# The last stage of a decoder layer on token tiles instead of feature chunks, and u blocks that end earlier

## The chip, the cores and the metric

One core of a Trainium2 chip runs the whole kernel. The metric is the device time of one execution in microseconds. The kernel before takes 2055.36 us (median of 3 runs, 2055.13 to 2056.61).

## What is computed

One step of one decoder layer for 544 tokens (512 of a prompt, 8 samples of 4) with 1024 features, all in 32-bit floats. Cut to what matters here:

```
x = x + merged @ w_out                      # two mixers, merged by gates
x = x + peer_ffn(rmsnorm(x, g_ffn), peer_wq, peer_keys, expert_u, expert_v)
ple_gate = sigmoid(rmsnorm(x, g_ple) @ w_ple_gate)   # 1024 x 1024
x = x + (p @ w_ple) * ple_gate                       # p: 544 x 256, w_ple: 256 x 1024
y = rmsnorm(x, g_final)
```

peer_ffn picks, for each token and each of 8 heads, the best 16 of 128 x 128 experts by two lists of 128 scores, and adds gate * gelu(h . u) * v over the picked rows of expert_u and expert_v.

## The kernel before, in words

**Numbers.** A product of two 32-bit matrices is three passes of TensorE over a high and a low part. `split` (L122 to L124) makes the parts: ScalarE (ACT) copies the high one (L123), VectorE (DVE) subtracts it (L124). A weight row that is loaded takes a raw buffer, then a high and a low one, in rings (`wload`, L128).

**Layout.** Up to the end, x lies with features on partitions: `x1` is 128 x 8 x 544, eight chunks of features. The sums of the experts lie with tokens on partitions.

**Stages, in us of the span.** Until about 657 the mixers, their merge and w_out. From there one block, "peer", whose order on every engine is set by a planner of the toolchain that plays the program through with its own costs (`schedule_with_timeline_sim`); the order below is what it made, and the engines run it strictly in that order.

1. *Queries and choice.* x1 is written to DRAM (`x1s`, five DMAs of POOL, L871), since its memory is reused. The norm of x1 (g_ffn) is split; 16 query columns wq are multiplied (`pj`, L917), turned into scores `psc` (L938), copied by ACT (`sc`, L939), and DVE takes the best 16 (`top16`). 16 transposes `ph` make token rows `htok` and `hsam` (L903 to L908). The transposes and the scores share two PSUM buffers (tag "mx"). Then DVE chooses among the pairs (`select`) and makes the gates with TensorE (`oa`, `ob`, `pg`, L1070 to L1088); the gates go to DRAM and come back as `gg`.
2. *Experts of the first 384 tokens, densely.* A u block multiplies 128 rows of expert_u by the normed x (24 matmuls `pu`, L967 to L970); 65 such blocks are made early, 63 late. The main loop has 128 steps j: a step loads one block of expert_v (`vraw`), splits it (`whi`, `wlo`) and the weights (`wgh`, `wgl`), and adds 18 matmuls of 512 columns into `pacc` (L1195), which fills six PSUM banks. The late u blocks are spread over the steps by `nlate * (j + 1) / LATE`, LATE = 127.
3. *Experts of the other 160 tokens, by gathered rows.* 320 times POOL gathers one row per token into one of 4 buffers `rows` (L1109) and DVE multiplies it (L1117, `jk`) or adds it (L1127, `accg`: `accs[0]` for 128 tokens, `accs[1]` for the samples). The steps lie between those of the main loop.
4. *The last stage.* x1 comes back from DRAM. The sums of each token tile are copied by ACT (`ot`, L1257), transposed in groups of four by TensorE (`pt`, L1250) and added to x1 (L1252); `accs` too, the samples by a small matmul with `sel` (L1289). Then, for two halves of 272 tokens: norm with g_ple (squares on ACT, their sum over partitions by TensorE, `pn`), eight chunks c with 24 matmuls each (`pj`, L1304: weights stationary, 272 tokens moving), sigmoid, times `pw` = p @ w_ple (L1266), added to x1; then the final norm and four output DMAs. Each w_ple_gate chunk is loaded and split twice, once for each half (16 loads).

Of the kernel before, what the change touches and what calls it, by code (L numbers as in the profile page):

```python
# [56 lines left out]
def step_kernel(ctx: ExitStack, tc: tile.TileContext, xT, pT, pk, wab, win, wbr, wout, wq, keysT, eu, eur, ev,  # L57
                wple, wpg, sh, sd, scv, yT, o_hp, o_dp, o_cv, o_hs, o_ds, gdram, ysp, gsp, x1s, asp, usp):
# [1172 lines left out]
    def tile_(tag, bufs, shape, dt=F32):
        return lp.tile(shape, dt, name=tag, tag=tag, bufs=bufs)

    yo0 = [tile_("yo", NYO, [128, 2, HT]) for _ in range(2)]
    tile_("xn3", NXN, [128, HT])
    tile_("sg2", 2, [128, HT])
    ph = tile_("fh", 2, [128, 2, T], F32R)
    pl = tile_("fl", 2, [128, 2, T], F32R)
    NRAW, NHI = TW
    wp = wr = tail.enter_context(tc.tile_pool(name="wpt", bufs=2, side="right", reuse_waits="tile"))  # L1240
    wpl = [wload(wple[i]) for i in range(2)]

    for k in range(2):
        nc.sync.dma_start(yo0[k].rearrange("p a b -> p (a b)"), pT[:, k])
        split(ph[:, k], pl[:, k], yo0[k].rearrange("p a b -> p (a b)"))

    def residual(t, ot, k0):
        p = psu.tile([128, 512], F32, name="pt", tag="pu").rearrange("p (a b) -> p a b", a=4)
        for k in range(4):
            PE.transpose(p[:, k], ot[:, k * 128:(k + 1) * 128], ident)  # L1250
        xc = x1[:, k0:k0 + 4, t * 128:(t + 1) * 128]
        V.tensor_add(xc, xc, p)  # L1252

    for t in range(3):
        for k0 in range(0, 8, 4):
            ot = ots[k0 // 4]
            S.activation(ot, pacc[t][:, k0 // 4], AF.Copy)  # L1257
            residual(t, ot, k0)
    for c in range(8):
        wh, wl = wpl[c // 4]  # L1260
        for hf in range(2):
            p = psu.tile([128, 512], F32, name="pw", tag="pu")
            for k in range(2):
                w_ = 2 * (c % 4) + k
                for j, (a, b) in enumerate(((wh, ph), (wh, pl), (wl, ph))):
                    PE.matmul(p[:, :HT], a[:, w_], b[:, k, HS[hf]], start=(k == 0 and j == 0), stop=(k == 1 and j == 2))  # L1266
            S.activation(pw[:, c, HS[hf]], p[:, :HT], AF.Copy)
# [1 line left out]
    psj = tail.enter_context(tc.tile_pool(name="psj2", bufs=4, space=PSUM, reuse_waits="tile"))
    pn = tail.enter_context(tc.tile_pool(name="pn2", bufs=2, space=PSUM, side="right", reuse_waits="tile"))  # L1270


    def norm(i):
        xs = x1[:, :, HS[i]]
        r = rms_rstd(x2p, pn.tile([128, 512], F32, name="pn", tag="pn").rearrange("p (a b) -> p a b", a=1),
                     lambda k: xs[:, k], 8, 0)
        return xs, r

    parts = []
    for i in range(2):  # L1280
        if i == 1:
            for k0 in range(0, 8, 4):
                residual(3, accs[0][:, k0 * 128:k0 * 128 + 512], k0)
            for k0 in range(0, 8, 4):
                p = psu.tile([128, 512], F32, name="pts", tag="pu")[:, :4 * NS].rearrange("p (a b) -> p a b", a=4)
                for k in range(4):
                    PE.matmul(p[:, k], accs[1][:, (k0 + k) * 128:(k0 + k + 1) * 128], sel, start=True, stop=True)
                xc = x1[:, k0:k0 + 4, TP:]
                V.tensor_add(xc, xc, p)  # L1289
        xs, r2 = norm(i)  # L1290
        hh = tile_("fh", 2, [128, 8, HT], F32R)
        hl = tile_("fl", 2, [128, 8, HT], F32R)
        for k in range(8):
            xn = tile_("xn3", NXN, [128, HT])
            V.scalar_tensor_tensor(xn, xs[:, k], par("g_ple", k), r2, op0=OP.mult, op1=OP.mult)
            split(hh[:, k], hl[:, k], xn)
# [104 lines left out]
```

## Time and profile before

| what | us |
|---|---|
| median of 3 runs | 2055.36 (2055.13 to 2056.61) |
| the profiled execution, its own time | 2064.72 |
| its span | 2062.6 |
| PE, DVE, ACT, POOL busy | 1982.7, 1702.2, 1031.5, 516.3 |
| last product of the main loop ends | 1946.6 |
| from there to the end of the span | 116.0 |

PE is TensorE's matmuls, PEld its weight loads, SP the engine that issues most DMAs. In a timeline a row gives start, duration, engine, line, operation, the tile written and those read, and what ended the idle time before it. A matmul's duration holds its way through the array, so the pace is the distance between starts. Where a group waits, the engine named behind the arrow is the one whose result came last.

### The profile page before, as it was taken

What the parts mean: (1) busy time and instruction counts of PE and PEld (TensorE: products, weight loads), DVE (VectorE), ACT (ScalarE), POOL (GpSimd) and SP (SyncE); (2) the same over time, 40 slices, a digit from 0 to 9 for tenths busy, and PEclk for the clock granted to TensorE, in tenths of its full rate; (3) what the DMA queues carried; (4) which work ended last, traced back from release to release, by engine and by line L of the source; (5) the groups of instructions that cost most, each with busy time, mean ns of one, the idle gap of its engine ahead of it and who ended that gap; (6) DMA issues with size and microseconds to landing.
All of it is one profiled execution on the core that took longest, in us unless ns stands there. A gap on an engine that the chain in (4) does not pass through costs nothing.

```text
span 2062.6 us, 34654 instructions
## 1 busy us (share of the span) xinstructions
PE 1982.7 (96%) x12292; PEld 1838.5 (89%) x12292; DVE 1702.2 (83%) x4579; ACT 1031.5 (50%) x1720; POOL 516.3 (25%) x509
## 2 busy tenths in 40 slices
PE   6899999999999999999999899999999999999887
PEld 6898988989998999999999888888888888888777
DVE  7687978876566799999999789888888788887877
ACT  5657576663534446765666433333333333333354
POOL 0001010010100001213332255543343344454510
PEclk9999999989999999999999999999999999999978
DMA  4323443434755238999999899999999999999843
GB/s 165 108 103 137 149 151 124 166 139 167 266 196 199 70 100 199 252 263 347 384 379 349 279 353 352 338 354 342 343 341 335 343 339 357 323 335 321 319 147 125
DMA packets 189420, 518.86 MB, mean 252 GB/s; under 512 B 18608, under 2 KB 72240, under 8 KB 189120
## 3 DMA queue, kind: packets, MB, share of 16 engines
q1 hardware_dynamic: 132384, 311.70, 42.8%
q0 software_dynamic: 56864, 204.96, 29.2%
q8 instruction: 96, 1.57, 0.3%
q14 instruction: 76, 0.62, 0.1%
HBM read 455.80 MB, written 60.79 MB: 250 GB/s over the span
## 4 chain that ended last, share of the span: by engine, by line
PE 83%; DVE 5%; DMA 4%; issue 3%; ACT 2%; POOL 1%; SPq 0%; DVEq 0%; ACTq 0%; POOLq 0%
PE pacc L1195 23%; PE pj L166 14%; PE pu L968 8%; PE pu L967 8%; PE pu L970 8%; PE pj L917 5%; PE pg L1084 4%; PE pj L1304 2%; DMA lraw<-in_eu 1%; DMA rows<-in_ev,idxs 1%; PE pmb L554 1%; PE pma L349 1%; PE pmb L545 1%; DMA usp<-lraw 1%; POOL rows L1109 1%
## 5 line engine op out<-in xcount | busy, mean ns | idle before, releaser
L967 PE MATMUL pu<-hh,whi 128*128 128x384 f32 x1024 | 346.1, 338 | 2.6 <-ACT act L978 2.6
L968 PE MATMUL pu<-hl,whi 128*128 128x384 f32 x1024 | 345.7, 338 | 0.0
L1109 POOL DMA_INDIRECT rows<-in_eur,idxs x160 | 215.0, 1344 | 291.5 <-DVE jk L1117 258.4
L124 DVE TENSOR_TENSOR wlo<-wraw,whi 128x1024 fp32r<-128x1024 f32 x169 | 206.3, 1221 | 76.0 <-ACT whi L123 66.1
L123 ACT ACTIVATE whi<-wraw 128x1024 fp32r<-128x1024 f32 x169 | 178.5, 1057 | 162.8 <-PE pj L166 85.1
L1109 POOL DMA_INDIRECT rows<-in_ev,idxs x160 | 203.2, 1270 | 226.4 <-DVE accg L1127 189.6
L1127 DVE SCALAR_TENSOR_TENSOR accg<-rows,wts,accg 128x1024 f32<-128x1024 f32 x158 | 202.2, 1280 | 14.5 <-DMA rows<-in_ev,idxs 14.1
L1195 PE MATMUL pacc<-whi,wgl 128*128 128x512 f32 x768 | 197.5, 392 | 5.3 <-DVE wgl L124 5.2
L970 PE MATMUL pu<-hh,wlo 128*128 128x384 f32 x1024 | 202.4, 336 | 0.0
L967 PEld LDWEIGHTS pu<-hh,whi 128*128 128x128 f32 x1024 | 192.5, 188 | 6.0 <-ACT act L978 3.6
L1195 PE MATMUL pacc<-whi,wgh 128*128 128x512 f32 x768 | 196.6, 391 | 0.2 <-ACT wgh L123 0.2
L1195 PE MATMUL pacc<-wlo,wgh 128*128 128x512 f32 x768 | 196.2, 391 | 0.0
L968 PEld LDWEIGHTS pu<-hl,whi 128*128 128x128 f32 x1024 | 192.4, 188 | 2.4
L124 DVE TENSOR_TENSOR wlo<-vraw,whi 128x1024 fp32r<-128x1024 f32 x128 | 156.5, 1223 | 34.5 <-ACT whi L123 29.3
L123 ACT ACTIVATE whi<-vraw 128x1024 fp32r<-128x1024 f32 x128 | 133.9, 1053 | 98.8 <-PE pacc L1195 72.2
L166 PE MATMUL pj<-xh,whi 128*128 128x272 f32 x768 | 176.6, 304 | 4.2 <-ACT sg L692 2.8
L970 PEld LDWEIGHTS pu<-hh,wlo 128*128 128x128 f32 x1024 | 178.7, 188 | 0.1
L1195 PEld LDWEIGHTS pacc<-whi,wgl 128*128 128x128 f32 x768 | 144.8, 189 | 37.2 <-DVE wgl L124 6.1
L166 PE MATMUL pj<-xh,wlo 128*128 128x272 f32 x768 | 175.4, 302 | 0.5 <-DVE wlo L124 0.5
L166 PE MATMUL pj<-xl,whi 128*128 128x272 f32 x768 | 174.4, 301 | 0.2 <-DVE xl L124 0.2
L1195 PEld LDWEIGHTS pacc<-wlo,wgh 128*128 128x128 f32 x768 | 144.9, 189 | 30.2
L1195 PEld LDWEIGHTS pacc<-whi,wgh 128*128 128x128 f32 x768 | 143.3, 188 | 27.0 <-ACT wgh L123 0.5
(488 smaller groups left out, 4326.0 us busy)
## 6 DMA issues: line engine op xcount, KB each, us to landing
wraw<-in_eu SPq DMA_DIRECT2D x128, 512.0 KB, 6.4
vraw<-in_ev SPq DMA_DIRECT2D x128, 512.0 KB, 6.4
wraw<-in_win SPq DMA_DIRECT2D x48, 512.0 KB, 3.6
gg<-gdram SPq DMA_DIRECT2D x25, 768.0 KB, 8.0
gdram<-go SPq DMA_DIRECT2D x36, 512.0 KB, 9.4
lraw<-in_eu SPq DMA_DIRECT2D x34, 512.0 KB, 4.0
usp<-lraw SPq DMA_DIRECT2D x34, 512.0 KB, 2.6
wlo<-usp SPq DMA_DIRECT2D x34, 512.0 KB, 7.7
```

What stands on the lines that cost most here:

```text
L123: S.activation(hi, src, AF.Copy)
L124: return V.tensor_sub(lo, src, hi.bitcast(F32))
L166: PE.matmul(ps[:, hf, :HT], a, b[:, HS[hf]], start=(i == 0 and j == 0), stop=(i == n - 1 and j == 2))
L917: PE.matmul(p[:, i, :HT], w_[:, k], x_[:, k, :HT], start=(k == 0 and j == 0), stop=(k == 7 and j == 2))
L967: PE.matmul(ps[:, :ND], wh[:, k], hh[:, k], start=(k == 0), stop=False)
L968: PE.matmul(ps[:, :ND], wh[:, k], hl[:, k], start=False, stop=False)
L970: PE.matmul(ps[:, :ND], wl[:, k], hh[:, k], start=False, stop=(k == 7))
L1084: PE.matmul(p[:, j], A[:, j], B[:, j], start=True, stop=True)
L1109: G.indirect_dma_start(out=r, out_offset=None, in_=src, in_offset=bass.IndirectOffsetOnAxis(ap=idx, axis=0))
L1127: V.scalar_tensor_tensor(accs[i], r, wts[i][:, k:k + 1], accs[i], op0=OP.mult, op1=OP.add)
L1195: PE.matmul(pacc[t][:, hf], w_[:, ts], v_[:, hf * 512:(hf + 1) * 512], start=(j == 0 and i == 0), stop=(j == 127 and i == 2))
L1304: PE.matmul(ps, a[:, k], b[:, k], start=(k == 0 and j == 0), stop=(k == 7 and j == 2))
```

## The change

It has three parts. Constants: LATE is 110 (the late u blocks are spread over steps 0 to 109, and the last 17 steps are products alone), and the last stage's weights have a ring of two raw buffers (TW = 2).

In the first stage x1 is written to DRAM with tokens on partitions: 40 transposes `px` into the "mx" buffers, ten ACT copies into `htok` or `hsam` (which are free until the token rows are made), ten DMAs of POOL.

In the last stage five tiles of tokens (128, 128, 128, 128, 32) are worked on, with features along the free axis. The sums are added to x1 straight from PSUM or from `accs`; a norm's sum of squares comes from one ACT operation with an accumulator; the normed tile is transposed in two groups of four and split; the normed tokens are stationary, and rows of w_ple and w_ple_gate of 512 columns move. Each of the ten weight rows is loaded and split once and kept. The norms run two tiles ahead of the outputs; there are five output DMAs; g_ple and g_final come as rows of 1 MB (`grow`).

```diff
-LATE = 127
+LATE = 110
-TW = 3, 2
+TW = 2
...
-    for t in range(5):
-        G.dma_start(x1s[t, :, :, :min(128, T - t * 128)], x1[:, :, t * 128:min(T, t * 128 + 128)])
...
+    for t in range(5):
+        n = min(128, T - t * 128)
+        for i in range(2):
+            p = pst.tile([128, 4, 128], F32, name="px", tag="mx")
+            for k in range(4):
+                PE.transpose(p[:n, k], x1[:, 4 * i + k, t * 128:t * 128 + n], ident)
+            xq = (htok, hsam)[t % 2][:n, i * 512:i * 512 + 512]
+            S.activation(xq.rearrange("p (a b) -> p a b", a=4), p[:n], AF.Copy)
+            G.dma_start(x1s[t, :n, i * 512:i * 512 + 512], xq)
...
     with tc.issue_after(loads[XL].ins):
         for t in range(5):
-            n = min(128, T - t * 128)
-            nc.sync.dma_start(x1[:, :, t * 128:t * 128 + n], x1s[t, :, :, :n])
+            nc.sync.dma_start(x1[:NT[t], t], x1s[t, :NT[t]])
+
+    def parts(src):
+
+        raw = tile_("wraw", TW, [128, 1024], F32, wt)
+        nc.sync.dma_start(raw, src)
+        hi = tile_("wth", 10, [128, 1024], F32R, wt)
+        lo = tile_("wtl", 10, [128, 1024], F32R, wt)
+        split(hi, lo, raw)
+        return hi, lo
+
+    for k in range(2):
+        raw = tile_("wraw", TW, [128, 1024], F32, wt)
+        nc.sync.dma_start(raw[:, :T], pT[:, k])
+        split(ph[:, k], pl[:, k], raw[:, :T])
+    wpl = [parts(wple[k]) for k in range(2)]
+    wgt = [parts(wpg[k]) for k in range(8)]
...
+    def residual(t):
+        n = NT[t]
+        for i in range(2):
+            c = slice(512 * i, 512 * i + 512)
+            if t < 3:
+                add = pacc[t][:, i]
+            elif t == 3:
+                add = accs[0][:, c]
+            else:
+                add = psu.tile([128, 512], F32, name="pts", tag="pu")[:NS]
+                PE.matmul(add, sel, accs[1][:, c], start=True, stop=True)
+            V.tensor_add(x1[:n, t, c], x1[:n, t, c], add)
+
+    def normed(t):
+
+        n = NT[t]
+        x = x1[:n, t]
+        xs = tile_("xs", 2, [128, 1024])
+        V.scalar_tensor_tensor(xs[:n], x, rstd(x, n, xs[:n]), gw[:n, 0], op0=OP.mult, op1=OP.mult)
...
+                PE.transpose(p[:, k, :n], xs[:n, c:c + 128], ident[:n, :n])
+            split(hi[:, 4 * i:4 * i + 4, :n], lo[:, 4 * i:4 * i + 4, :n], p[:, :, :n])
+        return hi[:, :, :n], lo[:, :, :n]
+
+    def mm_t(ps, xh_, xl_, ws):
+
+        for k, (wh, wl) in enumerate(ws):
+            for j, (a, b) in enumerate(((xh_[:, k], wh), (xl_[:, k], wh), (xh_[:, k], wl))):
+                for i in range(2):
+                    PE.matmul(ps[:, i], a, b[:, 512 * i:512 * i + 512], start=(k == 0 and j == 0),
+                              stop=(k == len(ws) - 1 and j == 2))
...
+    def last(t, pw, hi, lo):
+        n = NT[t]
+        p = psj.tile([128, 2, 512], F32, name="pj", tag="pj")[:n]
+        mm_t(p, hi, lo, wgt)
+        x = x1[:n, t]
+        for i in range(2):
+            c = slice(512 * i, 512 * i + 512)
+            sg = tile_("sg", 2, [128, 512])[:n]
+            S.activation(sg, p[:, i], AF.Sigmoid)
+            V.tensor_mul(sg, sg, pw[:, i])
+            V.tensor_add(x[:, c], x[:, c], sg)
+        yo = tile_("yo", 2, [128, 1024])[:n]
+        V.scalar_tensor_tensor(yo, x, rstd(x, n, yo), gw[:n, 1], op0=OP.mult, op1=OP.mult)
+        nc.sync.dma_start(yT[t * 128:t * 128 + n], yo)
...
+    xn_ = [ready(0), ready(1)]
+    pw_ = [embed(0)]
+    for t in range(5):
+        if t < 3:
+            xn_.append(ready(t + 2))
+        if t < 4:
+            pw_.append(embed(t + 1))
+        last(t, pw_[t], *xn_[t])
```

Where the planner put things. DVE, from the split of the last block of expert_v, before:

```order
L124 TENSOR_TENSOR wlo<-vraw,whi 128x1024
...
L1117 SCALAR_TENSOR_TENSOR jk,dots_6854<-rows,hsam 128x1024
L1127 SCALAR_TENSOR_TENSOR accg_6858<-rows,wts_6856,accg_6858 128x1024
L1137 TENSOR_TENSOR wts_6856<-wts_6856,gte 128x16
L1127 SCALAR_TENSOR_TENSOR accg_6858<-rows,wts_6856,accg_6858 128x1024
L124 TENSOR_TENSOR wgl<-act,wgh 128x384
L1127 SCALAR_TENSOR_TENSOR accg_6858<-rows,wts_6856,accg_6858 128x1024 x2
L124 TENSOR_TENSOR wgl<-act,wgh 128x384
L1127 SCALAR_TENSOR_TENSOR accg_6858<-rows,wts_6856,accg_6858 128x1024 x5
L1228 COPY sel<-ident 32x32 x4
L1127 SCALAR_TENSOR_TENSOR accg_6858<-rows,wts_6856,accg_6858 128x1024
L1252 TENSOR_TENSOR x_13925<-x_13925,pt 128x4x128 x2
```

and the same place in the change, up to the first low half of a weight of the last stage:

```order
L124 TENSOR_TENSOR wlo<-vraw,whi 128x1024
L1135 SCALAR_TENSOR_TENSOR accg_6858<-rows,wts_6856,accg_6858 128x1024
L124 TENSOR_TENSOR wgl<-act,wgh 128x384
L1135 SCALAR_TENSOR_TENSOR accg_6858<-rows,wts_6856,accg_6858 128x1024 x2
L124 TENSOR_TENSOR wgl<-act,wgh 128x384
L1135 SCALAR_TENSOR_TENSOR accg_6858<-rows,wts_6856,accg_6858 128x1024 x2
L124 TENSOR_TENSOR wgl<-act,wgh 128x384
L1135 SCALAR_TENSOR_TENSOR accg_6858<-rows,wts_6856,accg_6858 128x1024 x8
L1287 TENSOR_TENSOR x_20833<-x_20833,pacc_13993 128x512 x2
...
L124 TENSOR_TENSOR pl<-wraw,ph 128x544 x2
L1135 SCALAR_TENSOR_TENSOR accg_6858<-rows,wts_6856,accg_6858 128x1024 x3
...
L124 TENSOR_TENSOR wtl<-wraw,wth 128x1024
```

Behind the last block's split, 13 gathered rows stand ahead of the first addition to x1 where 11 stood, and 18 are left in all where 22 were; in the elided part stand the six other additions to x1 of tiles 1 to 3 and two more gathered rows. The weights of the last stage begin behind the last gathered row.

SP, the loads of the last stage in the change, with what each waits for:

```order
L1238 DMA x_20833<-x1s 128x1024 x4
L1238 DMA x_20833<-x1s 32x1024
L1251 DMA wraw<-in_pT 128x544 [waits DMAHW6_49]
L1251 DMA wraw<-in_pT 128x544 [waits DMAHW7_49,DVE_49,PE_49]
L1243 DMA wraw<-in_wple 128x1024 [waits DMAHW6_49,DMAHW0_49,DVE_49]
L1243 DMA wraw<-in_wple 128x1024 [waits DMAHW7_49,DMAHW1_49,DVE_49]
L1256 DMA gw<-in_grow 128x2048 [waits DMAHW2_49]
L1243 DMA wraw<-in_wpg 128x1024 [waits DMAHW3_49,DMAHW0_49,DVE_49]
L1243 DMA wraw<-in_wpg 128x1024 [waits DMAHW4_49,DMAHW1_49,DVE_49]
```

Every weight waits for DVE's subtraction on the weight two places earlier, the first w_ple row for that on the first half of p.

PE, the end of the change's first stage: the five groups of transposes stand between query matmuls; here the fourth and the fifth, then the token rows and the first scores:

```order
L886 MATMUL px<-ident,x_6282 128x128 x8
L925 MATMUL pj<-hl,whi 128x272
...
L886 MATMUL px<-ident,x_6282 32x128 x8
L925 MATMUL pj<-hh_6885,wlo 128x272
...
L911 MATMUL ph<-ident,hf 128x128
L914 MATMUL ph<-ident,x_7181 128x128
...
L914 MATMUL ph<-ident,x_7230 128x128
L946 MATMUL psc<-kt,qT 128x128 x4
L949 MATMUL psc_7264<-kt,q_7253 128x128
```

The first scores stand behind 192 query matmuls, 40 `px` and 16 `ph`, where they stood behind 173 and 16 `ph`.

## Rows read from the trace of the kernel before

**Rows 1.** The page: the chain that ended last, by engine.

```profile
PE 83%; DVE 5%; DMA 4%; issue 3%; ACT 2%; POOL 1%; SPq 0%; DVEq 0%; ACTq 0%; POOLq 0%
```

**Rows 2.** Stages: length, then busy us of PE, PEld, DVE, ACT, POOL, clock, DMA.

```profile
697.00:800.00 103.00, 102.91 (x810) 102.45 (x809) 102.54 (x699) 46.74 (x72) 5.22 (x6) 1.00 0.40 108
...
1100.00:1150.00 50.00, 50.00 (x353) 50.00 (x353) 47.24 (x116) 33.87 (x82) 9.57 (x13) 1.00 0.91 305
1150.00:1175.00 25.00, 19.57 (x104) 16.69 (x103) 12.87 (x21) 8.26 (x14) 3.53 (x3) 0.93 0.92 307
...
1200.00:1900.00 700.00, 700.00 (x3390) 618.07 (x3389) 577.69 (x732) 253.83 (x345) 313.26 (x237) 1.00 0.93 341
...
1947.00:1963.00 16.00, 5.66 (x24) 4.13 (x22) 12.62 (x18) 6.33 (x11) 7.21 (x6) 0.58 0.96 367
...
1984.00:2050.00 66.00, 59.61 (x424) 57.67 (x423) 53.94 (x119) 40.45 (x75) 0.00 (x0) 0.92 0.34 113
```

**Rows 3.** What PE waited for, 640 to 1200: us, times, longest.

```profile
PE pacc L1195 <- DVE wgl L124: 5.2, 1, 5.2
PE pj L917 <- ACT whi L123: 3.7, 1, 3.7
```

**Rows 4.** What DVE waited for, 690 to 1150.

```profile
DVE oa L1070 <- PE pg L1084: 7.3, 9, 1.7
DVE vals L893 <- ACT sc L939: 3.4, 1, 3.4
```

**Rows 5.** DMA issues, 625 to 700: KB each, median us to landing.

```profile
x1s<-x POOLq DMA_DIRECT2D x4, 512.0 KB, 5.9
```

**Rows 6.** Timeline of PE about the last product, and the last gate matmul.

```profile
1945.23 1.53 PE L1195 MATMUL pacc<-wlo,wgh 128*128 128x512 f32 x6
1946.59 1.09 PE L1250 MATMUL pt<-ident,ot 128*128 128x128 f32 x8
...
2048.87 0.29 PE L1304 MATMUL pj<-fh,wlo 128*128 128x272 f32 x1
```

**Rows 7.** Timeline of DVE: last v split, first residual addition, last gathered row.

```profile
1930.48 1.23 DVE L124 TENSOR_TENSOR wlo<-vraw,whi 128x1024 fp32r<-128x1024 f32 x1 [0.31 <-issue]
...
1952.45 1.28 DVE L1127 SCALAR_TENSOR_TENSOR accg<-rows,wts,accg 128x1024 f32<-128x1024 f32 x1 [2.20 <-DMA rows<-in_ev,idxs]
1953.65 1.28 DVE L1252 TENSOR_TENSOR x<-x,pt 128x512 f32<-128x512 f32 x2
...
1978.20 1.28 DVE L1127 SCALAR_TENSOR_TENSOR accg<-rows,wts,accg 128x1024 f32<-128x1024 f32 x1 [0.34 <-DMA rows<-in_ev,idxs]
```

**Rows 8.** DMA issues, 1925 to the end: KB each, median us to landing.

```profile
wraw<-in_wpg SPq DMA_DIRECT2D x16, 512.0 KB, 3.5
...
rows<-in_ev,idxs POOLq DMA_INDIRECT x21, 5.7
```

**Rows 9.** Groups of ACT, 1930 to the end, and one of DVE: busy, mean ns.

```profile
L123 ACT ACTIVATE whi<-wraw 128x1024 fp32r<-128x1024 f32 x18 | 18.9, 1057 | 11.1 <-PE pj L1304 6.9 <-issue 3.3 <-PE pw L1266 0.7
...
L1257 ACT ACTIVATE ot<-pacc 128x512 f32<-128x512 f32 x6 | 3.4, 596 | 14.5 <-PE pt L1250 7.9 <-PE pacc L1195 6.7
...
L124 DVE TENSOR_TENSOR wlo<-wraw,whi 128x1024 fp32r<-128x1024 f32 x18 | 22.0, 1221 | 3.9 <-ACT whi L123 3.9
```

**Rows 10.** Two stretches behind TensorE's idle time, columns as in rows 2.

```profile
1963.00:1970.00 7.00, 6.32 (x24) 5.68 (x25) 6.97 (x10) 2.45 (x7) 3.52 (x4) 0.50 0.72 251
1970.00:1984.00 14.00, 12.26 (x93) 11.37 (x92) 10.77 (x19) 9.49 (x22) 2.69 (x2) 0.99 0.50 172
```

**Rows 11.** Timeline of ACT about one load of a function table.

```profile
1999.80 0.39 ACT L1306 ACTIVATE sg<-pj 128x272 f32<-128x272 f32 x1
2000.21 1.28 ACT L108 ACT_TABLE_LOAD   x1
2001.50 0.21 ACT L108 ACTIVATE rs<-rs 128x3 f32<-128x3 f32 x1
```

**Rows 12.** Timeline of DVE: its last work.

```profile
2055.72 3.36 DVE L1313 SCALAR_TENSOR_TENSOR yo<-x,pkt,pn 128x272 f32<-128x272 f32 x8 [1.56 <-PE pn L116]
```

More of the change, by code (lines that the diff above doesn't have):

```diff
@@ L1218, in step_kernel, with tile_ @@
     lts.close()
+    aps.close()
+    NT = (128, 128, 128, 128, NS)
+    wt = tail.enter_context(tc.tile_pool(name="wt", bufs=1, side="right", reuse_waits="tile"))
+    lp = tail.enter_context(tc.tile_pool(name="lp", bufs=2, reuse_waits="tile"))
+    def tile_(tag, bufs, shape, dt=F32, pool=None):
+        return (pool or lp).tile(shape, dt, name=tag, tag=tag, bufs=bufs)
+    x1 = wt.tile([128, 5, 1024], F32, name="x2")
+    ph = tile_("ph", 1, [128, 2, T], F32R, wt)
+    pl = tile_("pl", 1, [128, 2, T], F32R, wt)
@@ L1227, in step_kernel @@
+    for k in range(2):
[4 more added lines that the diff above has]
+    wgt = [parts(wpg[k]) for k in range(8)]
+    gw = tile_("gw", 1, [128, 2, 1024])
+    nc.sync.dma_start(gw, grow)
+    sel = tile_("sel", 1, [128, NS])
     for g in range(4):
         V.tensor_copy(sel[32 * g:32 * g + 32], ident[32 * g:32 * g + 32, 32 * g:32 * g + 32])
-    lp = tail.enter_context(tc.tile_pool(name="lp", bufs=2, side="right", reuse_waits="tile"))
@@ L1231, in tile_ @@
[L1231 to L1252, printed above, removed]
-    for t in range(3):
[L1255 to L1267, printed above, removed]
@@ L1268, in step_kernel @@
-    psas.close()
[L1269 to L1296, printed above, removed]
-        parts.append((hh, hl))
@@ L1298, in step_kernel, with rstd @@
-    for i, (hh, hl) in enumerate(parts):
-        for c in range(8):
-            wh, wl = wload(wpg[c])
-            ps = psj.tile([128, 512], F32, name="pj", tag="pj")[:, :HT]
-            for k in range(8):
-                for j, (a, b) in enumerate(((wh, hh), (wh, hl), (wl, hh))):
-                    PE.matmul(ps, a[:, k], b[:, k], start=(k == 0 and j == 0), stop=(k == 7 and j == 2))
-            sg = tile_("sg2", 2, [128, HT])
-            S.activation(sg, ps, AF.Sigmoid)
-            V.tensor_mul(sg, sg, pw[:, c, HS[i]])
-            V.tensor_add(x1[:, c, HS[i]], x1[:, c, HS[i]], sg)
-        xs, r3 = norm(i)
-        for k in range(0, 8, 2):
-            yo = tile_("yo", NYO, [128, 2, HT])
-            for m in range(2):
-                V.scalar_tensor_tensor(yo[:, m], xs[:, k + m], par("g_final", k + m), r3, op0=OP.mult, op1=OP.mult)
-            nc.sync.dma_start(yT[:, k:k + 2, HS[i]], yo)
+    def rstd(x, n, junk):
+        q = tile_("rs", 4, [128, 5, 1])
+        ss, ms, rt, r, y = (q[:n, i] for i in range(5))
+        S.activation(junk, x, AF.Square, accum_out=ss)
+        V.tensor_scalar(ms, ss, 1.0 / 1024, EPS, op0=OP.mult, op1=OP.add)
+        S.activation(rt, ms, AF.Sqrt)
+        V.reciprocal(r, rt)
+        V.tensor_mul(y, r, r)
+        V.tensor_mul(y, y, ms)
+        V.tensor_scalar(y, y, -0.5, 1.5, op0=OP.mult, op1=OP.add)
+        V.tensor_mul(r, r, y)
+        return r
@@ new lines, in embed @@
+    def embed(t):
+        n, s_ = NT[t], slice(t * 128, t * 128 + NT[t])
+        p = psj.tile([128, 2, 512], F32, name="pw", tag="pj")[:n]
+        mm_t(p, ph[:, :, s_], pl[:, :, s_], wpl)
+        pw = tile_("pw", 2, [128, 2, 512])[:n]
+        for i in range(2):
+            S.activation(pw[:, i], p[:, i], AF.Copy)
+        return pw
+    def last(t, pw, hi, lo):
[3 more added lines that the diff above has]
+        x = x1[:n, t]
+        for i in range(2):
+            c = slice(512 * i, 512 * i + 512)
[6 more added lines that the diff above has]
+        nc.sync.dma_start(yT[t * 128:t * 128 + n], yo)
@@ L1340, in layout @@
     wbr = np.concatenate([blocks(f["w_br_a"][0]), blocks(f["w_br_b"][0])], axis=2)
-    wple = blocks(f["w_ple"][0]).reshape(2, 4, 128, 2, 128).transpose(0, 2, 1, 3, 4)
     d = dict(
```

32 lines of the change are left out of this document (19 added, 13 removed).

## The prediction

> **What bounds the kernel now.** I read the chain first: 83% of it is TensorE (PE) [rows 1]. The windows by stage then show where PE is full and where it isn't [rows 2]: from 1200 to 1900 it is busy for 700 of 700 us, so the main loop ends when PE has done its matmuls, counted from when the loop can begin. Two places are not full. In 1150 to 1175 PE has 19.6 of 25, since the gates go through DRAM before the first products need them: one wait of 5.2 us [rows 3]. And after the last product, which ends at 1946.6 = E [rows 6], the rest takes 116.0 us of the span of 2062.6; PE is busy 5.7 of the first 16 us and 59.6 of 66 later [rows 2]. Ahead of both lies a stage where PE and DVE are full together: 102.9 and 102.5 of 103 us, and from 1100 to 1150 PE 50.0, DVE 47.2 of 50 [rows 2]. The waits say who is second there: DVE waits 7.3 us for PE's `pg`, PE never for DVE's gates [rows 4].
>
> So the change has three prices: what the first stage pays for x1 by tokens, whether the last 17 steps stay full, and the length of the tail behind E. All is summed against the profiled execution (2064.7, span 2062.6); the median of the runs, 2055.36, lies 9.4 below it, and I carry the difference over to it.
>
> **1. The first stage.** Added: 40 transposes, 8 of them 1.09 us [rows 6], so 5.4 us of PE; ten copies on ACT, 0.60 each by the nearest row, `ot` [rows 9], 6.0 us; ten POOL DMAs for five. The first scores stand behind the 40 transposes and 19 more query matmuls at 103/810 = 0.127 us [rows 2], 2.4 us: 7.8 us later. They also stand behind the token rows, which overwrite htok and hsam and so wait for the last x1s transfer. Before, such a transfer landed after 5.9 us [rows 5]; the last one carries 64 KB, and 22 query matmuls (2.8 us) lie between: 0 to 2 us more. DVE's top 16, which waits for the first scores already now [rows 4], begins 8 to 10 us later.
>
> What of this reaches E? The 7.3 us that DVE waits for `pg` are its slack, so a late DVE alone would cost 10 - 7.3 = 2.7. PE has no slack but its own waits in the query stage, 3.7 us for weights [rows 3], in which transposes can run: 5.4 - 3.7 = 1.7 at the least. If the planner's order ties the two, DVE's full 10 comes through. I take PE's own work, 5.5, and keep **+2 to +10**. The 5.4 us that PE idles in 1150 to 1175 give nothing back: they wait on the gates, which come late with DVE.
>
> **2. The main loop.** The same 63 late u blocks, 128 products and splits in another order: nothing, as PE stays full. In the last 17 steps DVE loses the u splits (1.22 each [rows 9]), and no u block's load lies between the gathers. The edge is the last three `wgl`: in the new order five gathered rows stand ahead of the last one. With three rows there already and the next ones 2.1 us apart (below), it is done about 5.5 us before E and needed 4.1 us before (a step is 18 matmuls, 6 in 1.36 us [rows 6]). I take **+0.5**, 0 to 3.
>
> **3. The tail**, in us after E.
> (a) Gathered rows. The last v split waits for PE's weight buffers and stays at E - 16.1 [rows 7]. Before, 11 rows and the first addition took from 1930.5 to 1953.7: 2.1 us a row, where DVE needs 1.2; it is the way DVE, POOL, transfer (5.7 us [rows 8]), through 4 buffers, that takes the time. In the change 13 rows come first: -16.1 + 1.2 + 12 x 2.1 + 1.3 = +11.6. Bounds: 2.3 if every row is there (13 x 1.2, three `wgl` of about 0.55, the split), 15 if the turn takes an eighth longer.
> (b) Behind them on DVE, up to the first low half of a weight: 8 additions to x1 at 0.64 [rows 7], five rows at 1.2, two halves of p at about 0.65 (half a weight's), `sel` 0.9: 13.2. So 24.8.
> (c) Weights. The ring has two buffers, and a load is issued when DVE is done with the one two places earlier: 3.5 landing [rows 8], 1.06 ACT, 1.22 DVE [rows 9], some 0.3 of handing over: 6.1 us for two. The w_ple rows are done about 3.6 behind (b), the eight others four pairs later: 3.6 + 24.4 = 28.0. The last weight is split at 52.8. In that time PE has 94 matmuls of 0.227 and 24 transposes, 24.6 us, to do in some 28.
> (d) What stands behind the last weight in PE's order: 194 matmuls, 44.0; 16 transposes 2.2; two `sel` matmuls, 1.8 by my estimate from the same rate at a quarter: 48.0. So 100.8.
> (e) From the last gate matmul to the end 13.5 us before [rows 6]. The last scaling becomes one operation of 1.28 in place of 3.36 [rows 12], the two turns through PE's `pn` go (about 1.5), the sigmoid, product and sum are on 512 columns (about 1.6 more): 11.5. So 112.3. The end holds one change of ACT's function table. In the trace it costs its load alone: 2000.21 it starts, 0.02 behind the sigmoid, and 1.28 later the square root starts [rows 11]. The Trainium skill ("ScalarE: Activation LUTs", "What ACT_TABLE_LOAD costs") adds a drain of about 1.38 us to the load, 2.66 in all; by that the sum would be 1.4 higher. No drain shows in this trace, so the measurement decides, and I keep 1.28.
> (f) Clock. PE idles from E to about 24. After 1947 its granted clock fell to 0.58, and it stayed at half (the 1.2 GHz level) for 7 us of work, then was full [rows 2, 10]. Of 3.5 us lost so, (c) covers most: +2, 0 to 4. So **114.3**, against 116.0: **-1.7**.
>
> Bounds of the tail: (a) -9.3 to +3.4, (c) and (e) 2 each way, (f) as said: -10 to +6 when not all fall on one side.
>
> **Sum:** 5.5 + 0.5 - 1.7 = +4.3; 2064.7 + 4.3 = 2069.0 for a profiled execution, 2055.4 + 4.3 = 2059.7, say **2060** for the median. Its own range is 2052 to 2067. A measurement can tell 0.2% here, 4.1 us, from no change: this stands on that edge.
>
> **The rivals.**
> *Faster: the rows are there in time.* The place is DVE's 13 rows. No u block loads in the last 17 steps, and POOL may run the buffers full. If rows come every 1.3 us, (a) is 2.3 and the whole 4.3 - 9.3 = -5.0, about 2050; 2048 with +3.5 for the first stage. It decides from a pace of 1.4 us a row. For it: the DMA share is 0.93 in the loop [rows 2] and 0.72 and 0.50 where the loop's loads have ended [rows 10]. Against it: the very last row of before still waited for its transfer [rows 7], with nothing of the loop beside it, so it is the turn through four buffers, not load. But no other term of the tail is as uncertain, and (c) may be shorter too. 0.28.
> *Level: the first stage is hidden.* Transposes run in PE's waits, and DVE's 7.3 us take the later start [rows 3, 4]: +2, and the sum is +0.8, about 2056. For it the two waits; against it the 100% of both engines after 697. 0.10.
> *Slower: the clock stays low.* While weights come one in 3 us, a tile's six matmuls for each last 1.4, and PE waits between. If the clock stays at half all through (c), its 24.6 us are 49 and end 21 later than 28; half of that is +10, 2069. It decides where the bursts do not bring the clock back before the last weight. For it: 0.58 in 1947 to 1963, where PE worked 5.7 of 16 us [rows 2]. Against it: at half clock the bursts double and nearly join, and behind 7 us of such work the clock was full [rows 10]. The Trainium skill ("TensorE: Matmul & The Clock Gate", "HAM oscillation — how this bites in real kernels") describes this very case, tiles whose matmuls are shorter than the wait for the next load, each starting cold. By that rule this rival comes true; the trace agrees that idle time drops the clock, and shows the return too. 0.14.
> That norms do not run ahead, because the tile's norm waits behind gathered rows and weights on DVE, is part of the forecast: the change doesn't get there what it says.
>
> **Chances.** Forecast 0.48 (faster 0.02, same 0.14, slower 0.32); rows in time 0.28 (0.23, 0.05, 0); hidden 0.10 (0.03, 0.07, 0); clock 0.14 (all slower). Together faster 0.28, same 0.26, slower 0.46. The range takes in the faster rival to 2047 and the slower to 2070.
>
> **What would show it.** In the changed profile: the first scores 8 to 10 us later than 695; E later by some 6; the first addition to x1 about 11 us after E, the last weight split about 53 after; PE full from there for 48 us; the granted clock at half from about 10 to 30 us after E. The forecast is wrong if E has not moved, if the 13 rows are through within 5 us of E, if a weight takes over 3.5 us or under 2.5, or if PE waits between the last tiles.

## The result, and the profile after

The change makes the kernel slower by half a per cent. Over 19 runs each the median is 2068.94 us (2058.60 to 2075.14), and 2056.61 us (2049.13 to 2063.51) before: a ratio of 1.0051 (1.0036 to 1.0065), which is 10.5 us (7.4 to 13.4); the medians themselves are 12.3 apart. One execution in all, of the change without the transposes, ran at a granted clock of 0.56 and took 3271 us; it is left out of every figure below.

The two profiled executions differ by less: 2069.97 us with a span of 2068.0 now, 2064.72 with 2062.6 before. That lies ahead of the change, and is chance, as second profiles of both show (below). The first query matmul, the first place where the programs differ (I call it M), starts at 660.41 before and at 652.72 now:

```profile
652.72 0.39 PE L925 MATMUL pj<-hh,whi 128*128 128x272 f32 x1 [3.65 <-ACT whi L123]
```

So every time below is counted from M, or from E, the end of the last product.

| us | before | after | difference |
|---|---|---|---|
| M | 660.4 | 652.7 | -7.7 |
| M to DVE's first top 16 | 37.05 | 46.92 | +9.9 |
| M to the first product of the main loop | 497.9 | 506.8 | +8.9 |
| M to E | 1286.2 | 1294.0 | +7.8 |
| E to the first addition to x1 | 7.1 | 11.3 | +4.2 |
| E to the end (the tail) | 116.0 | 121.3 | +5.3 |

**First stage.** DVE starts its choice 9.9 us later. M and the first top 16 before, then the first top 16 in the change (652.72 + 46.92):

```profile
660.41 0.60 PE L917 MATMUL pj<-hh,whi 128*128 128x272 f32 x1 [3.65 <-ACT whi L123]
697.46 0.88 DVE L893 MAX8 vals<-sc 128x8 f32<-128x128 f32 x4 [3.42 <-ACT sc L939]
699.64 0.87 DVE L901 MAX8 vals<-sc 128x8 f32<-128x128 f32 x4 [1.93 <-ACT sc L947]
```

Most of that comes through: the gates are late, the first product is 8.9 later, E 7.8. The waits of PE (640 to 1950) and of DVE (690 to 1200) in the changed kernel: what waited and for what, us in all, times, longest.

```profile
PE pacc L1200 <- DVE wgl L124: 3.6, 1, 3.6
```

```profile
DVE oa L1078 <- PE pg L1092: 5.6, 8, 1.7
```

PE's wait for the gates shrank from 5.2 [rows 3] to 3.6, DVE's for `pg` from 7.3 [rows 4] to 5.6. So at most 1.6 and 1.7 us of a delay of 9.9 were absorbed in these two waits. Even that is not sure: profiled again, PE's wait is 3.6 before and 4.1 in the change, DVE's 7.2 and 6.8.

**Tail.** The timeline of DVE: the last split of expert_v, the last four of the 13 rows, the first addition, and the first and the last low half of a weight.

```profile
1930.82 1.23 DVE L124 TENSOR_TENSOR wlo<-vraw,whi 128x1024 fp32r<-128x1024 f32 x1
...
1952.55 3.93 DVE L1135 SCALAR_TENSOR_TENSOR accg<-rows,wts,accg 128x1024 f32<-128x1024 f32 x3 [2.47 <-DMA rows<-in_ev,idxs]
1956.81 1.28 DVE L1135 SCALAR_TENSOR_TENSOR accg<-rows,wts,accg 128x1024 f32<-128x1024 f32 x1 [0.34 <-DMA rows<-in_ev,idxs]
1958.01 2.47 DVE L1287 TENSOR_TENSOR x<-x,pacc 128x512 f32<-128x512 f32 x4
...
1971.67 1.23 DVE L124 TENSOR_TENSOR wtl<-wraw,wth 128x1024 fp32r<-128x1024 f32 x1 [0.47 <-ACT wth L123]
...
2001.80 1.23 DVE L124 TENSOR_TENSOR wtl<-wraw,wth 128x1024 fp32r<-128x1024 f32 x1 [2.01 <-ACT wth L123]
```

The timeline of PE, with E at 1945.36 + 1.36 = 1946.7:

```profile
1945.36 1.52 PE L1200 MATMUL pacc<-wlo,wgh 128*128 128x512 f32 x6
1971.69 1.22 PE L1310 MATMUL pw<-wth,ph 128*128 128x512 f32 x2 [24.82 <-ACT wth L123]
...
1974.42 1.04 PE L1310 MATMUL pw<-wth,pl 128*128 128x512 f32 x2
...
1977.16 0.62 PE L1310 MATMUL pw<-wth,ph 128*128 128x512 f32 x2
...
1985.14 1.22 PE L1310 MATMUL pj<-wth,fh 128*128 128x512 f32 x2 [5.08 <-ACT fh L123]
...
1987.86 1.05 PE L1310 MATMUL pw<-wtl,ph 128*128 128x512 f32 x2
...
2056.38 0.61 PE L1310 MATMUL pj<-wtl,fh 128*32 128x512 f32 x2
```

PE stands still for 24.8 us until the first weight is there, and for 5.1 us until tile 0's normed tokens `fh` are split. From 1985.14 on it never waits again. The second wait is ACT's order. The copy of `fh` stands behind the high half of a weight whose load is not there yet (4.1 us) and four copies of `pw`:

```profile
1981.60 1.06 ACT L123 ACTIVATE wth<-wraw 128x1024 fp32r<-128x1024 f32 x1 [4.12 <-DMA wraw<-in_wpg]
1982.56 2.04 ACT L1324 ACTIVATE pw<-pw 128x512 f32<-128x512 f32 x4
1984.47 0.62 ACT L123 ACTIVATE fh<-pt 128x512 fp32r<-128x512 f32 x1
```

The stretches of the tail, columns as in [rows 2]:

```profile
1947.00:1963.00 16.00, 0.00 (x0) 0.00 (x0) 12.62 (x14) 1.81 (x3) 9.58 (x8) 0.64 0.81 276
1963.00:1984.00 21.00, 8.36 (x32) 6.63 (x32) 16.71 (x30) 8.09 (x13) 0.00 (x0) 0.66 0.63 221
1984.00:2050.00 66.00, 64.86 (x283) 48.42 (x284) 35.79 (x76) 35.54 (x58) 0.00 (x0) 0.96 0.18 64
```

In the first 16 us PE does nothing, where it had 5.7 us of transposes before [rows 2]. From 1984 it is full (64.9 of 66) where it had gaps. The change concentrates the tail's matrix work, yet starts it later.

### The profile page after: what moved, and what is told of

Same layout as the page of the kernel before. It is cut to its first block, busy times and chain, and to the rows that moved or that the text cites. A ratio compares the mean times of both kernels' runs of the same rounds, so it can differ in the third digit from the quotient of the medians.

```text
span 2068.0 us, 34164 instructions
## 1 busy us (share of the span) xinstructions
PE 1976.3 (96%) x12100; PEld 1813.9 (88%) x12100; DVE 1688.6 (82%) x4539; ACT 1030.2 (50%) x1696; POOL 514.3 (25%) x514
## 4 chain that ended last, share of the span: by engine, by line
PE 85%; DMA 5%; DVE 4%; ACT 3%; issue 2%; POOL 0%; SPq 0%; ACTq 0%; DVEq 0%; POOLq 0%
PE pacc L1200 24%; PE pj L166 14%; PE pu L976 9%; PE pu L975 9%; PE pu L978 9%; PE pj L925 5%; PE pg L1092 4%; PE pj L1310 3%; DMA lraw<-in_eu 1%; DMA rows<-in_ev,idxs 1%; PE pmb L554 1%; PE pmb L545 1%; PE pma L349 1%; DMA usp<-lraw 1%; PE psc L946 1%
## 5 line engine op out<-in xcount | busy, mean ns | idle before, releaser
L1117 POOL DMA_INDIRECT rows<-in_ev,idxs x160 | 213.0, 1331 | 266.5 <-DVE accg L1135 223.4
L1117 POOL DMA_INDIRECT rows<-in_eur,idxs x160 | 200.5, 1253 | 253.9 <-DVE jk L1125 211.1
L124 DVE TENSOR_TENSOR wlo<-wraw,whi 128x1024 fp32r<-128x1024 f32 x151 | 184.2, 1220 | 86.2 <-ACT whi L123 79.7
L123 ACT ACTIVATE whi<-wraw 128x1024 fp32r<-128x1024 f32 x151 | 159.5, 1056 | 139.2 <-PE pj L166 81.8
```

The source lines that it names most:

```text
L123: S.activation(hi, src, AF.Copy)
L124: return V.tensor_sub(lo, src, hi.bitcast(F32))
L1117: G.indirect_dma_start(out=r, out_offset=None, in_=src, in_offset=bass.IndirectOffsetOnAxis(ap=idx, axis=0))
```

## The experiments

The milestones of all the traces, in us: M, then from M to the first top 16, to the first product and to E, then from E to the first addition to x1 and to the end. Each is one profiled execution.

| kernel | M | top 16 | product | E | addition | tail |
|---|---|---|---|---|---|---|
| before | 660.4 | 37.1 | 497.9 | 1286.2 | 7.1 | 116.0 |
| before, profiled again | 655.4 | 37.1 | 498.0 | 1285.2 | 6.4 | 116.2 |
| before, LATE 110 | 657.2 | 37.9 | 498.8 | 1286.2 | 4.3 | 111.1 |
| before with the transposes | 651.9 | 45.7 | 505.5 | 1293.3 | 4.8 | 110.5 |
| before, DVE held up | 656.1 | 41.4 | 501.6 | 1292.6 | 4.3 | 117.0 |
| change | 652.7 | 46.9 | 506.8 | 1294.0 | 11.3 | 121.3 |
| change, profiled again | 655.4 | 45.8 | 505.6 | 1293.2 | 11.0 | 120.2 |
| change, LATE 127 | 649.8 | 45.7 | 505.5 | 1293.4 | 9.8 | 118.8 |
| change without the transposes | 651.4 | 38.3 | 499.2 | 1286.9 | 10.9 | 117.7 |
| change, 16 gathered samples | 654.2 | 45.8 | 505.5 | 1292.5 | -0.6 | 101.9 |
| change, tile of 32 left out | 657.3 | 47.0 | 507.4 | 1294.5 | 10.8 | 106.6 |
| change, p in its own buffers | 652.9 | 45.7 | 505.5 | 1293.4 | 12.5 | 123.8 |
| change, transposes later | 654.9 | 37.9 | 506.9 | 1297.6 | 10.3 | 119.3 |
| x1 turned behind the loop | 652.7 | 38.0 | 498.9 | 1286.1 | – | 130.1 |

### The parts one by one: the transposes, and LATE

The change without the 40 transposes:

```diff
+    for t in range(5):
+        ...
+        G.dma_start(d, x1[:, :, t * 128:t * 128 + n])
...
-                PE.transpose(p[:n, k], x1[:, 4 * i + k, t * 128:t * 128 + n], ident)
...
-            S.activation(xq.rearrange("p (a b) -> p a b", a=4), p[:n], AF.Copy)
-            G.dma_start(x1s[t, :n, i * 512:i * 512 + 512], xq)
```

> The change without its 40 transposes, ten copies and ten small DMAs: x1 goes to DRAM by five DMAs as before, so the residual that comes back is not turned to tokens on partitions (the output is not the layer's). Counted from the first query matmul, which lies before anything the change touches, to the last product (E), before takes 1286.2 us and the change 1294.0. Theory 'first stage' (the transposes put off the first scores and with them DVE's choice, which begins 37.0 us after the first query matmul before, 46.9 in the change): the choice begins at 37 again, E at 1286, the whole is 8 us shorter than the change, about 0.1% above the kernel before. Rival 'order of u blocks' (E is later since the last 17 steps lack u blocks): the choice begins earlier, but E stays at 1294 and the time at the change's.

Measured: 2056.75 us, ratio 0.9984 (0.9964 to 1.0003). E is at 1286.9 from M, 7.1 earlier than in the change. The other way round, before with the transposes, their copies and ten DMAs into a DRAM tensor that nothing reads:

```diff
+                PE.transpose(p[:n, k], x1[:, 4 * i + k, t * 128:t * 128 + n], ident)
+            xq = (htok, hsam)[t % 2][:n, i * 512:i * 512 + 512]
+            S.activation(xq.rearrange("p (a b) -> p a b", a=4), p[:n], AF.Copy)
+            G.dma_start(x1t[t, :n, i * 512:i * 512 + 512], xq)
```

> The kernel before with the change's transposes, copies and ten DMAs added, into a DRAM tensor of their own that nothing reads (its own five DMAs stay). Theory 'first stage': the choice begins 47 us after the first query matmul, E at 1294, the whole 8 us (0.4%) slower than before, the tail as before at 116. Rival 'order of u blocks': E within 2 us of 1286, no change in time.

Measured: 2060.70 us, ratio 1.0032 (1.0009 to 1.0055), E at 1293.3, 7.1 later than before. Put in or taken out, the transposes move E by the same 7.1 us, so that price belongs to them, with their copies and DMAs, and not to LATE or to the last stage. (That the two agree to the decimal is luck: E of one and the same kernel differs by up to 1.0 us from profile to profile.) The tail of this kernel, in which nothing was touched, is 110.5 instead of 116.0; why is not shown.

The traces also show where the price is paid. From 740 to 1145 us the kernels with and without the transposes run the same instructions in the same order on PE and on DVE. Counted from M, those of before with the transposes lie 7.0 to 7.5 us behind those of before (profiled again), from 80 us behind M all the way to the first product. So nothing in this stretch, where both engines are full, takes up the late start.

LATE by itself, in the change and before:

```diff
-LATE = 110
+LATE = 127
```

> The change with LATE at 127 again, one constant. Theory 'first stage': E stays at 1294, the tail within 2 us of the change's 121.3, the time is the change's. Rival 'order of u blocks': E falls by 6 or more towards 1286. Third way, that the earlier end of the u blocks was a gain inside the change: E or the tail gets longer by 3 or more.

```diff
-LATE = 127
+LATE = 110
```

> The kernel before with LATE 110 alone. Theory 'first stage': E within 1 us of 1286, the tail within 3 us of 116, no change in time. Rival 'order of u blocks': E at 1292 or later.

Measured: the change with 127 takes 2064.50 us, 1.0042 (1.0021 to 1.0064); before with 110 takes 2058.78, 0.9999 (0.9982 to 1.0016). E does not move in either (1293.4 and 1286.2). The 17 steps do nothing that can be seen there. In its one trace, before with 110 has a tail of 111.1 instead of 116.0; the times do not bear out a gain of 4.9 us.

### Does DVE have slack in the first stage?

Before, with 16 in-place multiplications by 1.0 on DVE ahead of the first top 16, and nothing more for PE:

```diff
+        if c == 0:
+            for _ in range(16):
+                V.tensor_scalar(sc, sc, 1.0, None, op0=OP.mult)
```

> The kernel before with 16 multiplications of the first scores by 1.0 in place, on DVE, ahead of the first search for the best 16: DVE begins the choice later by some 5 to 10 us (X), TensorE gets no work. Theory 'DVE carries it': E is later by 0.7 X or more. Theory 'TensorE's own work', where DVE's 7.3 us of waiting for the gates' matmuls are its slack: E is later by less than 0.3 X.

Measured (one execution, 2067.82 us): the top 16 begins 4.3 us later, the first product 3.7, E 6.4. DVE's waits for `pg` and PE's for the gates:

```profile
DVE oa L1073 <- PE pg L1087: 6.6, 9, 2.0
```

```profile
PE pacc L1198 <- DVE wgl L124: 8.5, 1, 8.5
PE pacc L1198 <- ACT wgh L123: 1.5, 1, 1.5
```

DVE still waits 6.6 us for `pg`, against 7.3 [rows 4], though it began 4.3 late: those waits took up next to nothing of the delay. What E lost beyond the first product, 2.7 us, lies in PE's wait for the gates behind it, 10.0 us in two waits, where it was 5.4 before (5.2 [rows 3] and 0.2). But this is not a delay of DVE alone. The planner made a new order for this kernel, which differs from before's on PE and on DVE in many places from 700 to 1200 us, so the 6.4 us are those of the delay and of the new order together.

So I tried to keep DVE's start and pay for the transposes later, one tile after each of the query columns 2 to 6:

```diff
+        if 2 <= c < 7:
+            t = c - 2
...
+                    PE.transpose(p[:n, k], x1[:, 4 * i + k, t * 128:t * 128 + n], ident)
+                xq = hf.rearrange("p a b -> p (a b)")[:n, (t % 2) * 1024 + i * 512:][:, :512]
```

> The change with its 40 transposes moved behind the third of the 16 query columns, one tile of tokens after each of columns 2 to 6, through memory of the normed x that is free by then: the same work, but the first scores do not wait for it (the choice begins 37 to 39 us after the first query matmul, as before). Theory 'DVE carries it' (the choice and the gates on DVE, begun 9 us late, are what put E off by 7): E is back at 1286 to 1288, the whole 6 to 7 us shorter than the change. Theory 'TensorE's own work' (the 5.4 us of transposes are simply more matmuls, which is how the prediction priced it): E at 1291 to 1293, the whole 1 to 2 us shorter than the change.

Measured: 2071.75 us, 1.0070 (1.0049 to 1.0091), the slowest of all. The first top 16 is back at 37.9, yet the first product comes at 506.9 and E at 1297.6. DVE's waits show it:

```profile
DVE vals L889 <- ACT sc L935: 10.9, 5, 3.4
```

It waited 3.4 once before [rows 4]; now 10.9 in five turns. The transposes and their copies go through the PSUM buffers of the scores, and can hold up the next scores each time. That this is the cause is argued and not isolated, since the planner's order differs in other places of the stage too. An early start of DVE is worth nothing if DVE is not fed behind it.

### The tail: rows, tile of 32, ring of p

With half of the samples' gathered steps:

```diff
-        yield from g_steps(1, hsam, 32)
+        yield from g_steps(1, hsam, 16)
```

> The change with 16 instead of 32 gathered rows per expert list of the sample tokens: half of their experts are left out, and DVE has no gathered row behind the main loop. Theory 'matmuls behind the rows': the 25 us that TensorE waits after the last product fall to about 13 (first addition within 2 us of E, first weight's low half at about 10 to 13), the tail falls by about 12 to 109. Rival 'loads': TensorE's wait is set by the two weights' way through the ring from E on, and the tail falls by less than 4.

Measured: 2048.26 us, 0.9945 (0.9927 to 0.9964); the first addition is at -0.6, the first low half of a weight at 11.9 and the tail 101.9, 19.4 us shorter. PE's waits from 1930 on:

```profile
PE pt L1301 <- DVE xs L1294: 8.5, 1, 8.5
PE pj L1310 <- ACT fh L123: 0.7, 1, 0.7
```

Of 24.8 + 5.1 us of waiting 8.5 + 0.7 are left, so the rows ahead of the first weight set when PE starts. The edit takes gathered work out of the main loop too, but E moved by only 0.7 to 1.5. It also takes out the five rows that stood behind the additions to x1, so the 19.4 us are not the price of the 13 rows alone.

Without gate and embedding of the tile of 32 tokens, 60 of 300 matmuls:

```diff
-    for t in range(5):
+    for t in range(4):
...
+    residual(4)
...
+    V.scalar_tensor_tensor(yo, x, rstd(x, NS, yo), gw[:NS, 1], op0=OP.mult, op1=OP.mult)
```

> The change without the gate and the embedding of its last tile, the 32 tokens of the samples: 60 of the tail's 300 matmuls, which each run as long as for 128 tokens, are left out (their output is then only the final norm of the residual). In the change's profile TensorE works without a gap from 1985 to 2057. Theory 'matmuls': the tail is TensorE's work behind its two waits, so it falls by 60 x 0.233 = 14 us, from 121 to about 107. Rival 'weights and gathered rows': the tail hangs on what DVE and the loads do, and falls by less than 5.

Measured: 2055.82 us, 0.9981 (0.9965 to 0.9997), the tail 106.6, 14.7 shorter. Sixty matmuls at the pace of the change's timeline (0.233, below) are 14.0, and the tile's eight transposes 0.6 (2044.34 to 2044.95). PE sets the end of the tail, and 32 stationary tokens cost as much as 128.

With two raw buffers of p's own, so that the weights don't queue behind p in the ring:

```diff
-        raw = tile_("wraw", TW, [128, 1024], F32, wt)
+        raw = tile_("praw", 2, [128, T], F32, wt)
```

> The change with two raw buffers of their own for p, so that the first two weights of the last stage need not wait until DVE has split p. Theory 'the ring keeps the weights back': the weights are there before DVE is past its rows, the first matmul behind E comes at 19 instead of 25, when p is split, and the 5 us wait for the first norm's high half goes with it; the tail is 115 to 117. Rival 'rows': everything still waits for DVE's gathered rows, the tail stays within 2 us of 121.

Measured: 2069.17 us, 1.0047 (1.0024 to 1.0070), the tail 123.8. The first weight was split 20.9 us after E instead of 24.9, but the tail got no shorter, so the theory that the ring is what costs the time fell. PE waited elsewhere:

```profile
PE pw L1310 <- DVE x L1287: 13.7, 1, 13.7
PE pt L1301 <- DVE xs L1294: 10.1, 1, 10.1
PE pw L1310 <- DVE pl L124: 5.3, 1, 5.3
```

Its first product needs PSUM that the additions to x1 release, and then the halves of p and the norm. All of them are DVE's, behind the gathered rows: 29.1 us in three waits.

### A version meant to beat both

x1 goes to DRAM as before, comes back with features on partitions (`xf`), and 24 matmuls with the identity add it into `pacc` behind the last product. The halves of p go through x's own memory, and the rings of `fh`, `fl` and `yo` are one buffer smaller:

```diff
+            for k in range(4):
+                PE.matmul(p[:, k * 128:k * 128 + 128], xf[:, 4 * i + k, t * 128:t * 128 + n], ident, start=t == 3,
+                          stop=k == 3 or t == 3)
...
-            V.tensor_add(x1[:n, t, c], x1[:n, t, c], add)
+            S.activation(x1[:n, t, c], p, AF.Copy)
```

> A version of the change without its first stage: x1 goes to DRAM and comes back with features on partitions, as before, and behind the last product 24 matmuls with the identity add it to the sums in PSUM (16 more serve the last two tiles); ACT copies the sums out, so three tiles do not wait for DVE's gathered rows, and p comes through x's own memory, so the weights load at once. Theory 'first stage and rows': E as before (1286 to 1287 after the first query matmul), first matmul of the last stage within 12 us of E, tail 103 to 108, the whole 5 to 10 us faster than before (ratio 0.995 to 0.998). Rival 'matmuls': TensorE's 300 matmuls and 40 more fill 85 us and the low clock adds 7, tail 115, no gain over before.

Measured: 2068.77 us, 1.0045 (1.0023 to 1.0066), a miss. The first stage is free again (E at 1286.1), but the tail is 130.1. The waits of PE, and SP's timeline:

```profile
PE pacc L1279 <- DMA xf<-x1s: 23.3, 1, 23.3
```

```profile
1952.27 1.46 SPq L1238 DMA_DIRECT2D wraw<-in_wpg  x2
1953.79 10.11 SPq L1233 DMA_DIRECT2D xf<-x1s  x5
```

The planner put the loads of `xf` behind weight loads on SP's queue, which wait for DVE. E is at 1938.8 here, and the first of them is issued 15 us later.

### A second profile of both

No edit.

> The kernel before, profiled a second time. The two first profiles differ by 5.3 us where the medians differ by 12.3; the first query matmul came at 660.4 in the one of before and between 650 and 657 in the others. Theory 'clock in the mixers' (the part ahead of any change runs between 650 and 660 from execution to execution, and the profile of before was a slow one): the first query matmul comes 3 to 10 us earlier than 660.4, the choice at 37 to 38.5 and E at 1286 to 1287 behind it again, the tail at 110 to 117. Rival 'the programs differ there': the first query matmul at 659 to 661 again.

> The change, profiled a second time, for the same question: the choice 45 to 47 us behind the first query matmul, E at 1293 to 1294.5, the tail 118 to 122; the first query matmul anywhere from 650 to 660 by theory 'clock in the mixers', 651 to 654 again by the rival.

Measured: 2058.95 and 2070.81 us. M is 655.4 in both, so the 7.7 us between the first two profiles belong to the execution and not to the kernel. The rest repeats within 1.2 us.

## Why the prediction was right or wrong

The sign held (slower), and so did the widest range (2047 to 2070). The time came out 9 us above the 2060, and above the forecast's own range of 2052 to 2067. That it lies below 2070 is luck: the range reached so far for the rival of the low clock, which did not happen. The sign is owed to the first stage; that of the tail was wrong by the traces. The steps:

**1. First stage, +5.5 (2 to 10).** Measured +7.1 for the transposes, +7.8 and +8.0 for the whole change in its two pairs of profiles: within the bounds, low by about 2, and for the wrong reason. The top 16 came 9.9 and 8.7 late, within the 8 to 10. The sentence that failed is "the 7.3 us that DVE waits for `pg` are its slack, so a late DVE alone would cost 10 - 7.3 = 2.7". Those waits covered next to nothing: of a top 16 that came 8.6 us late in before with the transposes, 7.0 to 7.5 were still there at every instruction up to the first product. PE's own 5.4 us of work is not the measure either: the later transposes, with the same work in another order, cost 11.4. "If the planner's order ties the two, DVE's full 10 comes through" was the better half of the sentence. Which of the two full engines holds the other in this stretch stays open, since the run that was to delay DVE alone got a new order. The rival in which the stage is hidden falls with it.

**2. Main loop, +0.5 (0 to 3).** Nothing, by both LATE runs. The last `wgl` was done 4.0 us before E and not 5.5 (1942.14 + 0.55), and PE did not wait for it.

**3. Tail, -1.7.** The traces show about +5. This is the step that failed.

| step, us after E | predicted | measured |
|---|---|---|
| (a) 13th row done | 11.6 | 11.3 |
| (b) first low half of a weight | 24.8 | 25.0 |
| (c) last weight split | 52.8 | 56.3 |
| (d) last gate matmul done | 100.8, with (f) 102.8 | 110.1 |
| (e) from there to the end | 11.5 | 11.2 |

(a), (b) and (e) are right to 0.3 us: the rows' turn of 2.1 us read from the trace of before held. (c) priced the ring of loads as if ACT were always free for them. The high half of the second w_ple row stood behind the squares of a norm and a load of ACT's function table, and a row of w_ple_gate landed 4.1 us after ACT was free for it (above):

```profile
1970.59 1.06 ACT L123 ACTIVATE wth<-wraw 128x1024 fp32r<-128x1024 f32 x1 [10.07 <-DMA wraw<-in_wple]
1971.55 1.04 ACT L1265 ACTIVATE xs<-x 128x1024 f32<-128x1024 f32 x1
...
1972.70 1.28 ACT L1267 ACT_TABLE_LOAD   x1
...
1974.10 1.04 ACT L123 ACTIVATE wth<-wraw 128x1024 fp32r<-128x1024 f32 x1
```

It also left out that the 1 MB of g_ple and g_final goes over the same queue as the weights. It and the w_ple rows took longer to land than the 3.5 of a w_ple_gate row; whether one slowed the other is not shown:

```profile
wraw<-in_wpg SPq DMA_DIRECT2D x8, 512.0 KB, 3.6
...
wraw<-in_wple SPq DMA_DIRECT2D x2, 512.0 KB, 4.9
gw<-in_grow SPq DMA_DIRECT2D x1, 1024.0 KB, 7.5
```

But (c) did not set the end. "PE has 94 matmuls of 0.227 and 24 transposes, 24.6 us, to do in some 28" is the step that failed, with the 194 of (d) behind it: PE's work behind the first weight was priced too low and then cut in two, as if the last weight set the end. By 2002.9, just before the split ended, PE had done 85, and 215 were left. From E + 25 on PE has 80.1 us of work and 5.1 of waiting, where I had 74.6 (24.6 + 48.0 + 2) and 3.4. Four things made this:
- the count. Five tiles by ten weight rows by three passes by two halves are 300 matmuls; 94 and 194 are 288. Twelve by 0.227 are 2.7 us.
- the pace. Between full rows of the last stage two matmuls take 0.465 to 0.47, so 0.233 each; 300 by 0.006 more are 1.8.
- the clock, 3.4 instead of 2 (below).
- the wait for `fh`, 5.1 us, which I had nowhere: I had PE waiting for weights, 3.4 us, and a tile's norm beside them. That is 1.7 more.

The 40 transposes gave some of it back: eight take 0.79 in the change's timeline (2000.20 to 2000.99), not 1.09, which was the length of a row, with the way through the array, and not the pace. So 1.5 us for all. The two `sel` matmuls, estimated at 1.8, took 2.0 (2031.35 to 2032.33 and 2032.68 to 2033.66). What remains, about 1 us, I can't place.

How the 10.5 us divide is sure for the transposes in the traces only. By the times, before with transposes is 6.6 us over before (1.9 to 11.3), which leaves some 4 for the tail; but the change without transposes is 3.3 *under* before (7.4 under to 0.6 over), which would leave none. In the traces the four kernels with the change's tail and all its work (both profiles, LATE 127, without transposes) have 117.7 to 121.3, the five with the old tail 110.5 to 117.0. The old tail itself differs by 6.5 us between kernels that leave it alone. So a longer tail is what I read, by some 5 us, while its share of the measured time stays open.

**The rivals.** "The rows are there in time" did not happen: the 13th row was done 11.3 us after E. The run with half the samples' steps shows that early rows would have been worth much: the first addition came 11.9 us earlier and the tail was 19.4 shorter, where the rival counted one for one. It is not quite the rival's case, which keeps all the rows. "The clock stays low" was not it either. Windows of the changed kernel about the two bursts that follow PE's waits:

```profile
1971.00:1975.00 4.00, 3.31 (x8) 2.66 (x9) 2.10 (x8) 3.97 (x6) 0.00 (x0) 0.50 0.74 268
1976.00:1980.00 4.00, 4.00 (x22) 3.19 (x20) 3.90 (x10) 1.06 (x1) 0.00 (x0) 1.00 0.38 129
1984.00:1988.00 4.00, 2.86 (x7) 2.28 (x8) 2.58 (x4) 4.00 (x8) 0.00 (x0) 0.50 0.37 131
1989.00:1993.00 4.00, 4.00 (x21) 3.25 (x20) 2.31 (x8) 1.55 (x2) 0.00 (x0) 1.00 0.61 214
```

The granted clock was 0.50, the 1.2 GHz level, at the head of each burst (1971.7 to 1975.3 and 1985.1 to 1988.7), and 1.00 soon after. There 16 matmuls took 7.2 us instead of 3.7 (16 by 0.233): 3.4 lost, 1.4 more than forecast, where the rival had +10. The Trainium skill ("TensorE: Matmul & The Clock Gate", "HAM oscillation — how this bites in real kernels") describes bursts that each start cold. By that rule both dips come, and the trace agrees; but they were two and not one for each tile, since PE never waited again after the second.

## What to carry to other kernels

An engine's wait for another is slack only if what it waits for does not in turn depend on the engine itself: test it by delaying that engine alone, and see that the order of the rest stays what it was. Count the matmuls of a new stage from its loops and check the sum before dividing them into "beside" and "behind" a wait. Where PE starts late and then never waits, the stage's length is the start plus all of PE's work, so 32 stationary tokens at the price of 128, and whatever stands on the in-order queue ahead of the first operand, count in full.

## What the runs showed of the hardware that was not expected

- A matmul with 32 stationary columns in use and 512 moving ones takes what one with 128 takes: in the change's timeline pairs of `128*32` start 0.45 to 0.47 us apart, as pairs of `128*128` do.
- TensorE's clock in the mixers differs from run to run of the same code. From 400 to 475 us it was 0.91 in the profile of before, 0.95 in that of the change and 1.00 in that of the change with LATE 127, and M came at 660.4, 652.7 and 649.8 us. In all 14 traces M lies between 649.8 and 660.4, a spread as large as the effect under study.
- A load of ACT's function table again cost its own length. The last one of the change, on ACT's timeline:

```profile
2061.18 0.18 ACT L1265 ACTIVATION_READ_ACCUMULATOR yo<-x 32x1 f32 x1
2061.38 1.28 ACT L1267 ACT_TABLE_LOAD   x1
2062.68 0.20 ACT L1267 ACTIVATE rs<-rs 32x1 f32<-32x1 f32 x1
```

It starts 0.02 us behind the accumulator's end and the square root 0.02 behind it. The drain of 1.38 us that the Trainium skill ("ScalarE: Activation LUTs", "What ACT_TABLE_LOAD costs") adds is not there, and the step from the last gate matmul to the end, costed without it, is one of those that held.
